# Recurrent projections: ScalarE in the written order, eight eviction tiles for the keys, squares in the keys' own tiles, decay weights in ring slots

## The chip, the cores and the metric

The kernel runs on one core of a Trainium2 chip. A core has five engines that run side by side and meet only through semaphores: TensorE (PE in the profile; PEld is its weight load), VectorE (DVE), ScalarE (ACT), GpSimd (POOL) and SyncE (SP), whose queue issues every DMA of this kernel. The metric is the device time of one execution in microseconds (us), taken as the median of several runs.

## What is computed

Two post-norm layers over 512 tokens of 1024 channels. Each layer is a half-step SwiGLU, a token mixer, and another half-step SwiGLU. The first mixer is a neighbourhood attention, the second a two-directional RWKV-7 recurrence. The change lies in the projections that feed the recurrence:

```python
xx = 0.5 * (x_prev + x_next) - x
xr, xw, xk, xv, xa, xg = (x + xx * mix[i] for i in range(6))
r = xr @ w_rkv[0]
k = xk @ w_rkv[1]
wl = w0 + tanh(xw @ w1) @ w2            # one per direction z
decay = exp(-exp(-softplus(-wl) - 0.5))
a = sigmoid(a0 + (xa @ a1) @ a2)
g = sigmoid(xg @ g1) @ g2
kk = (k * k_k) / norm(k * k_k)          # norm per head of 64 channels
```

## The kernel before, in words

**Numbers and tiles.** Activations lie with 128 channels on the partitions and the 512 tokens along a row, so 1024 channels are eight chunks, `c` or `o` = 0 to 7. To keep fp32 accuracy a large operand is split into a rounded part (ScalarE's copy to fp32r) and the rest (a subtraction on VectorE or GpSimd, line 276 after line 275). A product is then three matmuls, `mm3`, lines 285 to 287. Small products stay in plain fp32 (lines 676, 775, 781, 817).

**The stage.** `rwkv_project` runs once, between the third SwiGLU and the recurrence. It first mixes the keys' input into the split tiles `mk` (tag xT, two buffers), then:

1. multiplies the keys: eight weight blocks of 128 rows, each against all eight banks `acc[o]`; the last block finishes the banks one by one;
2. evicts each bank twice on ScalarE: `store` (line 705) copies it to an eviction tile from `evac`, which SyncE writes to `d_k`, and line 748 squares it into `sqs[o]` for the norm;
3. makes two low-rank products, `rank(0)` for the decay (`pw`) and `rank(1)` for `a` (`pa`), line 676;
4. applies a tanh to `pw` (line 752, which needs another activation table) and splits the result into `wh[z]` (lines 760 to 763);
5. splits the decay weights `w2[z]` (lines 719 to 723: a load, two roundings on ScalarE, two subtractions on VectorE, for z = 0 and 1);
6. multiplies the first 128 receptance channels, `receptance`, line 775: chunks 0 to 3, then the sums of squares `ss` per head (line 781, reading `sqs`), then chunks 4 to 7. Their inputs `t` come from VectorE (line 712) in four buffers of tag tmp;
7. multiplies the decays of direction 0 (`decays(0)`, lines 798 to 802: two matmuls, a tanh on ScalarE, a scaling on VectorE, a store to `d_lw`), the first part of the gate's second block (line 817), the decays of direction 1, the gate's hidden layer (`rank(2)`, then `tail`/`hidden`, lines 830 to 837), and four chunks of the gate itself (lines 841 to 846). `scan.begin` and `scan.front` (lines 1130 to 1420) are interleaved: they load `ah`, `k`, `r`, `lw`, `iv` back and prepare the first head pair of the recurrence.

After the stage the recurrence begins with matmuls of line 1113, whose operand `xs` SyncE loads behind the gate's four stores.

**What sets the order.** Inside `manual_schedule(engines=...)` the named engines run their instructions in the order in which the code issues them; for the others a scheduler chooses. In the block from line 735 on, PE and VectorE are manual (`MANUAL_MIX`), ScalarE is scheduled. SyncE and GpSimd are always scheduled. Each engine and SyncE's queue run strictly in their order, so an instruction that waits holds those behind it. A tile of a tag with n buffers waits until an earlier tile of the tag is no longer used. `ring` has 11 slots of 128 x 2048 elements, `raw` two per pool, with a second pool `spares` that alternates with it during this stage. `evac` goes round four tiles of 128 x 512 (one ring slot) during the keys' eviction and round eight from line 753 on.

## Time and profile before

| what | value |
|---|---|
| median of 3 runs | 2206.18 us (2203.84 to 2210.39) |
| the profiled execution: its time, its span | 2205.93 us, 2204.1 us |
| mean granted TensorE clock in it | 0.996 of full speed |
| PE busy | 2161.4 us |
| GpSimd, VectorE, ScalarE busy | 1398.9, 1056.8, 959.7 us |

The profile is one execution. Its time stands 0.25 us from the median of the runs, and 1.8 us of it lie outside the span. A row of the timeline gives an instruction or a run of like instructions: start, length, engine, line, output and input, and in brackets the idle time of its engine before it and what ended that. One plain fp32 matmul of 512 columns appears as two records. The granted clock is the share of TensorE's full clock that the hardware let through.

### The profile page before, as it was taken

How to read it: one execution, taken by the hardware profiler on the slowest of the kernel's cores; microseconds unless marked ns; L12 is line 12 of the kernel's file. 1: busy time of each engine (PE TensorE's matmuls, PEld its weight loads, DVE VectorE, ACT ScalarE, POOL GpSimd, SP SyncE). 2: the span in 40 equal slices, each digit the busy share in tenths (PEclk: the TensorE clock that was granted, in tenths of full speed). 3: DMA queues.
4: the chain of work that ended last, by engine and by line, in shares of the span. 5: the costliest groups of instructions: out<-in, count | busy, mean ns of one | idle time of the engine just before them, and what ended most of it. 6: DMA issues, size and time to landing. Idle time of an engine off the chain costs nothing.

```text
span 2204.1 us, 35069 instructions
## 1 busy us (share of the span) xinstructions
PE 2161.4 (98%) x13808; PEld 1698.6 (77%) x13808; DVE 1056.8 (48%) x1535; ACT 959.7 (44%) x1684; POOL 1398.9 (63%) x1226
## 2 busy tenths in 40 slices
PE   9999999999999999999999999999999999999998
PEld 8888888887888888888888875536666557888876
DVE  3223355367433333743333578635888545233345
ACT  3333345377333333443333443537777533333333
POOL 5988855555488877487888541045777713877753
PEclk9999999999999999999999999999999999999999
DMA  7444463432344444554444543864545653444443
GB/s 207 150 152 148 141 227 98 123 96 75 111 149 143 143 142 130 196 163 141 146 148 141 205 147 118 277 163 122 146 128 136 182 161 108 139 142 135 143 164 124
DMA packets 348628, 325.64 MB, mean 148 GB/s; under 512 B 48464, under 2 KB 277328, under 8 KB 348464
## 3 DMA queue, kind: packets, MB, share of 16 engines
q1 hardware_dynamic: 348464, 323.41, 47.5%
q8 instruction: 108, 1.77, 0.3%
q14 instruction: 56, 0.46, 0.1%
HBM read 261.22 MB, written 45.88 MB: 139 GB/s over the span
## 4 chain that ended last, share of the span: by engine, by line
PE 88%; DVE 3%; ACT 3%; DMA 2%; issue 2%; POOL 1%; SPq 1%; DVEq 0%; ACTq 0%; POOLq 0%
PE bank L286 17%; PE bank L285 17%; PE bank L287 17%; PE bank L921 16%; PE bank L348 4%; PE a L1113 3%; PE g L1441 1%; PE y L1113 1%; PE bank L1306 1%; PE m L1113 1%; PE m L1627 1%; PE g L1113 1%; PE c L1609 1%; PE g L1464 1%; PE y L1640 1%
## 5 line engine op out<-in xcount | busy, mean ns | idle before, releaser
L276 POOL TENSOR_TENSOR w<-raw,w 128x1024 fp32r<-128x1024 f32 x198 | 486.0, 2456 | 228.7 <-ACT w L275 221.3
L285 PE MATMUL bank<-xT,w 128*128 128x512 f32 x1264 | 493.9, 391 | 0.0
L286 PE MATMUL bank<-xT,w 128*128 128x512 f32 x1264 | 492.8, 390 | 0.0
L287 PE MATMUL bank<-xT,w 128*128 128x512 f32 x1264 | 492.4, 390 | 0.0
L275 ACT ACTIVATE w<-raw 128x1024 fp32r<-128x1024 f32 x202 | 213.2, 1058 | 318.8 <-POOL ts L892 131.0
L492 DVE SCALAR_TENSOR_TENSOR ar<-bank,tmp 128x512 f32<-128x512 f32 x88 | 60.9, 692 | 570.0 <-PE bank L287 558.4
L287 PEld LDWEIGHTS bank<-xT,w 128*128 128x128 f32 x1264 | 237.4, 188 | 49.5
L285 PEld LDWEIGHTS bank<-xT,w 128*128 128x128 f32 x1264 | 237.4, 188 | 48.8
L286 PEld LDWEIGHTS bank<-xT,w 128*128 128x128 f32 x1264 | 237.5, 188 | 48.1
L921 PE MATMUL bank<-wx,an 128*128 128x512 f32 x792 | 187.6, 390 | 0.0
L921 PEld LDWEIGHTS bank<-wx,an 128*128 128x128 f32 x792 | 148.7, 188 | 31.1
L921 PE MATMUL bank<-w,ring 128*128 128x512 f32 x720 | 169.1, 391 | 2.7 <-POOL w L276 2.6
L276 POOL TENSOR_TENSOR wx<-ra,wx 128x512 fp32r<-128x512 f32 x132 | 167.0, 1291 | 3.0 <-ACT wx L275 3.0
L1548 POOL TENSOR_TENSOR tm<-qs,zs 128x126 f32<-128x126 f32 (+22 forms) x248 | 106.1, 428 | 95.5 <-issue 41.1
L276 DVE TENSOR_TENSOR ring<-ar,ring 128x1024 fp32r<-128x1024 f32 x44 | 124.8, 2837 | 83.3 <-ACT ring L275 83.2
L921 PEld LDWEIGHTS bank<-w,ring 128*128 128x128 f32 x720 | 134.9, 188 | 32.3 <-POOL w L276 3.5
L490 ACT ACTIVATE tmp<-bank 128x512 f32<-128x512 f32 x88 | 52.6, 597 | 229.9 <-PE bank L287 229.9
L1550 POOL TENSOR_TENSOR zs<-zs,tm 128x126 f32<-128x126 f32 (+22 forms) x248 | 113.1, 456 | 19.4
L275 ACT ACTIVATE wx<-ra 128x512 fp32r<-128x512 f32 x132 | 82.8, 633 | 79.6 <-PE bank L921 66.6
L276 POOL TENSOR_TENSOR ring<-raw,ring 128x1024 fp32r<-128x1024 f32 x24 | 59.0, 2465 | 82.2 <-ACT ring L275 82.2
L498 DVE TENSOR_TENSOR ar<-ar 128x256 f32<-128x256 f32 x44 | 92.5, 2102 | 1.5
L276 POOL TENSOR_TENSOR w<-xT,w 128x1024 fp32r<-128x1024 f32 x25 | 65.2, 2614 | 42.5 <-ACT w L275 42.5
(358 smaller groups left out, 3976.1 us busy)
## 6 DMA issues: line engine op xcount, KB each, us to landing
raw<-in_ffn_w_in_dram SPq DMA_DIRECT2D x176, 512.0 KB, 3.9
ra<-in_ffn_w_out_dram SPq DMA_DIRECT2D x44, 1024.0 KB, 4.9
xT<-d_late SPq DMA_DIRECT2D x29, 512.0 KB, 5.1
raw<-in_w_qkv_dram SPq DMA_DIRECT2D x24, 512.0 KB, 3.9
xT<-in_ffn_w_out_dram SPq DMA_DIRECT2D x23, 512.0 KB, 4.4
d_late<-ts SPq DMA_DIRECT2D x44, 256.0 KB, 3.3
d_late<-ra SPq DMA_DIRECT2D x44, 256.0 KB, 2.0
xs<-ar SPq DMA_DIRECT2D x64, 128.0 KB, 2.6
```

Of the source, the lines that this page charges most:

```text
L275: self.hi = self.nc.scalar.activation(h, raw, AF.Copy).ins
L276: self.lo = (eng or self.nc.vector).tensor_tensor(l, raw, h.bitcast(F32), ALU.subtract).ins
L285: nc.tensor.matmul(out, wh, xh, start=start, stop=False)
L286: nc.tensor.matmul(out, wh, xl, start=False, stop=False)
L287: nc.tensor.matmul(out, wl, xh, start=False, stop=stop)
L348: nc.tensor.matmul(acc[t, h], a, u[:, i, h * 512 : (h + 1) * 512], start=first and n == 0, stop=last and n == 2)
L492: nc.vector.scalar_tensor_tensor(raw[:, 3:7:3] if j else raw[:, 0:8:7], halves_of(pu), 0.5, halves_of(s), ALU.mult, ALU.mult)
L498: nc.vector.tensor_tensor(a(2), a(1), a(0), ALU.subtract)
L921: self.nc.tensor.matmul(acc, lhs, u[:, i], start=bool(first) and m == 0, stop=last and m == 2, skip_group_check=more)
L1113: self.nc.tensor.matmul(out[hs], w[:, hs], x, start=start, stop=stop)
L1548: nc.gpsimd.tensor_tensor(tv, qs[:, s, 0:s].rearrange("p (a o) -> p a o", o=1).broadcast_to([P, s, n]), zs[:, s : s + 1, c0:].broadcast_to ...
L1550: nc.gpsimd.tensor_tensor(zs[:, 0:s, c0:], zs[:, 0:s, c0:], tv, ALU.add)
```

## The change

ScalarE joins the manual engines of the block, so it runs its instructions as the code issues them. The second eviction tile set is appended ahead of the keys' eviction, so that `evac` goes round eight tiles there. The squares go into one of the two xT buffers that held the keys' split operand, and `rows[2]` (`grows`) into the other, as before. The two decay weight units take ring slots, and the unit for z = 0 is issued ahead of the tanh, after the mixing of `low_rank(2, ...)`; the one for z = 1 follows the split of `wh`. The eviction of `pa` and the load and split of `ug` (the gate's weights) move ahead of the second half of the receptance.

```diff
-            with self.tc.manual_schedule(engines=MANUAL_MIX):
+            with self.tc.manual_schedule(engines=MANUAL_SCAN):
...
-                sqs = [q[:, c, :] for q in (quarters(), quarters()) for c in range(4)]
+                spent = [self.sb.tile([P, 4 * D], F32, name="xT", tag="xT", bufs=2) for _ in range(2)]
+                sqs, grows = ([x[:, c * S : (c + 1) * S] for c in range(ND)] for x in spent)
+                rows.append(grows)
+                evs.append(quarters())
                 for o in range(ND):
                     store(dram["rkv"][1][:, o, :], acc[o])
                     nc.scalar.activation(sqs[o], acc[o], AF.Square, scale=self.col(C_KK, o))
 
                 pw = rank(0)
+                rs = raws(0, dram["xr"])
+                soon = [next(rs) for _ in range(ND // 2)]
+                low_rank(2, g1[:, :P], 5)
+                decay_units = [decay_unit(self.ring(), 0)]
                 wt = evac()
                 nc.scalar.activation(wt, pw, AF.Tanh)
-                evs.append(quarters())
-                rs = raws(0, dram["xr"])
-                soon = [next(rs) for _ in range(ND // 2)]
-                units, grows = self.sb.tile([P, 4 * D], F32R, name="xT", tag="xT", bufs=2), self.sb.tile([P, 4 * D], F32, name="xT", tag="xT", bufs=2)
-                rows.append([grows[:, c * S : (c + 1) * S] for c in range(ND)])
-                low_rank(2, g1[:, :P], 5)
                 for z in range(2):
...
-                decay_units = [decay_unit(units[:, z * 2 * D : (z + 1) * 2 * D], z) for z in range(2)]
+                decay_units.append(decay_unit(self.ring(), 1))
...
                 pa = rank(1)
+                store(dram["ah"], pa)
...
-                store(dram["ah"], pa)
+                ug = self.load_unit(g2[:P, :], ring=True, eng=nc.vector)
                 receptance(soon)
...
-                ug = self.load_unit(g2[:P, :], ring=True, eng=nc.vector)
```

PE's and GpSimd's instructions stand as before. VectorE takes the two subtractions of the decay weights for z = 0 ahead of the split of `wh` instead of behind it, and the subtraction of `ug` ahead of the eight mixings into `xraw` instead of behind the reciprocal. On SyncE's queue the load of `ug`'s weights moves ahead of the first stores to `d_xr`, and the eight stores to `d_k` stand together. ScalarE is shown at three places. In the rows an underscore number is a buffer's; line numbers after the change are one less up to line 741 or differ by a few below it.

The first place is the end of the keys' eviction, before the change (`bank_10008` to `bank_10010` are the last three banks of keys, `raw_10303` and `raw_10309` the decay weights of z = 0 and 1):

```order
L705 ACTIVATE ring_9918<-bank_10008 128x512
L748 ACTIVATE ring_10236<-bank_10008,cols_246 128x512
L720 ACTIVATE xT_10284<-raw_10303 128x1024
L722 ACTIVATE xT_10284<-raw_10303 64x1024
L705 ACTIVATE ring_9918<-bank_10009 128x512
L748 ACTIVATE ring_10236<-bank_10009,cols_246 128x512
L720 ACTIVATE xT_10284<-raw_10309 128x1024
L722 ACTIVATE xT_10284<-raw_10309 64x1024
L705 ACTIVATE ring_9918<-bank_10010 128x512
L748 ACTIVATE ring_10236<-bank_10010,cols_246 128x512
L752 ACT_TABLE_LOAD
L752 ACTIVATE ring_9918<-bank_10261 128x512
```

The same place after the change (`raw_10293` is now z = 0's weights, `bank_10318` is `pa`):

```order
L704 ACTIVATE ring_10237<-bank_10009 128x512
L750 ACTIVATE xT_10235<-bank_10009,cols_246 128x512
L704 ACTIVATE ring_9918<-bank_10010 128x512
L750 ACTIVATE xT_10235<-bank_10010,cols_246 128x512
L719 ACTIVATE ring_10292<-raw_10293 128x1024
L721 ACTIVATE ring_10292<-raw_10293 64x1024
L758 ACT_TABLE_LOAD
L758 ACTIVATE ring_9918<-bank_10262 128x512
L762 ACTIVATE ring_9919<-ring_9918 64x512 x4
L719 ACTIVATE ring_10308<-raw_10309 128x1024
L721 ACTIVATE ring_10308<-raw_10309 64x1024
L704 ACTIVATE ring_9918<-bank_10318 128x512
```

The roundings for z = 0 moved from between the evictions to behind them, and those for z = 1 behind the tanh and its split.

The second place is the end of the receptance, before (`bank_10327` is `pr`, `bank_10385` and `bank_10391` the first decays, `ring_10462` is `ug`):

```order
L705 ACTIVATE ring_9918<-bank_10327 128x512
L275 ACTIVATE ah_10373<-ring_10374 128x512
L280 ACTIVATE gt_10371<-raw_10467 96x512
L800 ACTIVATE ring_10271<-bank_10385 128x512
L275 ACTIVATE ring_10462<-raw_10461 128x1024
L280 ACTIVATE ring_10466<-raw_10467 96x512
L800 ACTIVATE ring_10271<-bank_10391 128x512
```

After the change these roundings stand between the two directions' decays (`bank_10432` is the last of z = 0, `bank_10473` the first of z = 1):

```order
L801 ACTIVATE ring_9918<-bank_10432 128x512
L819 ACTIVATE ring_10315<-bank_10448 128x512
L274 ACTIVATE ah_10378<-ring_10379 128x512
L274 ACTIVATE a2u_10460<-a2r_10446 128x256
L279 ACTIVATE ring_10466<-raw_10467 96x512
L279 ACTIVATE gt_10376<-raw_10467 96x512
L801 ACTIVATE ring_10237<-bank_10473 128x512
```

The rounding of `ug` is gone from here; it now stands right behind the eviction of `pa`.

The third place is the gate's hidden layer, before (`gh` is its first 128 rows, `ring_9920` its split):

```order
L800 ACTIVATE ring_10271<-bank_10515 128x512
L832 ACTIVATE gh_10370<-bank_10525 128x512
L280 ACTIVATE gt_10371<-ring_10315 96x512
L1386 ACTIVATE ring_10374<-bank_10544 128x512
L1388 ACTIVATE ring_10374<-bank_10544 128x512
L1393 ACTIVATE ring_10374<-bank_10551,cols_246 128x512
L1407 ACTIVATE pcs_10458<-ring_10374 64x8 x2
L275 ACTIVATE ring_9920<-gh_10370 128x512
```

After:

```order
L832 ACTIVATE ring_10315<-bank_10523 96x512
L279 ACTIVATE gt_10376<-ring_10315 96x512
L832 ACTIVATE gh_10375<-bank_10525 128x512
L274 ACTIVATE ring_9920<-gh_10375 128x512
L1386 ACTIVATE ring_10379<-bank_10544 128x512
L1388 ACTIVATE ring_10379<-bank_10544 128x512
L1393 ACTIVATE ring_10379<-bank_10551,cols_246 128x512
L1407 ACTIVATE pcs_10463<-ring_10379 64x8 x2
```

The rounding of the hidden layer now follows its activation directly; five instructions of the recurrence's preparation stand behind it.

More of the change, by code (lines that the diff above doesn't have):

```diff
@@ L50 @@
 MANUAL = {mybir.EngineType.PE}
-MANUAL_MIX = {mybir.EngineType.PE, mybir.EngineType.DVE}
 MANUAL_NORM = {mybir.EngineType.Activation, mybir.EngineType.DVE}
```

## The prediction

> **What bounds the kernel now.** The first page first: the span and the busy shares.

> ```profile
> span 2204.1 us, 35069 instructions
> PE 2161.4 (98%) x13808; PEld 1698.6 (77%) x13808; DVE 1056.8 (48%) x1535; ACT 959.7 (44%) x1684; POOL 1398.9 (63%) x1226
> ```

> TensorE is busy for all but 42.7 us, so a faster other engine can only win what PE idles, or what its clock loses. No PE instruction is added, removed or moved. Next the waits, between the end of the keys' products and the first matmuls of the recurrence.

> ```profile
> PE bank L775 <- DVE tmp L712: 4.8, 1, 4.8
> PE y L1113 <- DMA xs<-in_w_rkv_dram: 2.4, 1, 2.4
> PE bank L285 <- ACT ring L275: 2.1, 1, 2.1
> PE bank L817 <- ACT ring L800: 0.6, 1, 0.6
> ```

> Each row has the total, the count and the longest wait in us. PE's longest is for VectorE's `tmp`. The timelines of ScalarE, VectorE and PE show what makes those late:

> ```profile
> 1346.90 0.60 ACT L705 ACTIVATE ring<-bank 128x512 f32<-128x512 f32 x1 [8.73 <-PE bank L287]
> 1350.54 0.74 ACT L748 ACTIVATE ring<-bank,cols 128x512 f32<-128x512 f32 x1
> 1356.31 0.60 ACT L705 ACTIVATE ring<-bank 128x512 f32<-128x512 f32 x1 [5.04 <-DMA d_k<-ring]
> 1358.42 1.07 ACT L720 ACTIVATE xT<-raw 128x1024 fp32r<-128x1024 f32 x1
> 1364.43 1.28 ACT L752 ACT_TABLE_LOAD   x1
> 1365.73 0.60 ACT L752 ACTIVATE ring<-bank 128x512 f32<-128x512 f32 x1
> 1366.36 2.57 ACT L762 ACTIVATE ring<-ring 64x512 fp32r<-64x512 f32 x4
> ...
> 1353.26 5.39 DVE L681 SCALAR_TENSOR_TENSOR xT<-ring,cols,xraw 128x512 f32<-128x512 f32 x8
> 1369.68 1.22 DVE L721 TENSOR_TENSOR xT<-raw,xT 64x1024 fp32r<-64x1024 f32 x1
> 1374.63 2.74 DVE L712 SCALAR_TENSOR_TENSOR tmp<-ring,cols,xraw 128x512 f32<-128x512 f32 x4
> ...
> 1351.47 13.89 PE L676 MATMUL bank<-ring 128*128 128x512 f32 x32
> 1365.20 3.60 PE L775 MATMUL bank<-tmp,wr 128*128 128x512 f32 x8
> 1368.72 1.92 PE L781 MATMUL bank<-ring,heads 128*32 128x512 f32 x16
> 1375.44 5.93 PE L775 MATMUL bank<-tmp,wr 128*128 128x512 f32 x8 [4.79 <-DVE tmp L712]
> 1380.80 4.24 PE L798 MATMUL bank<-xT,ring 128*128 128x512 f32 x16
> ```

> Four pairs of copy and square fill the four eviction tiles by 1351.28; ScalarE then stands still until a store to `d_k` has landed. With two decay roundings in between, the tanh comes at 1365.73, though `rank(0)` had ended halfway through the 13.89 us of line 676, at 1358.42. VectorE holds its four `tmp` mixings behind the tanh's split and four subtractions, and PE waits 4.79 us. Eight records of line 775 then take 5.93 us instead of 3.60: the clock.

> ```profile
> 1375.40:1379.40 4.00, 3.96 (x5) 1.85 (x6) 4.00 (x7) 0.00 (x0) 0.00 (x0) 0.50 0.79 217
> 1402.90:1407.30 4.40, 4.17 (x10) 3.11 (x11) 4.33 (x8) 1.72 (x3) 0.00 (x0) 0.61 0.75 251
> 1415.90:1418.30 2.40, 0.07 (x2) 0.00 (x0) 2.30 (x4) 2.21 (x6) 0.00 (x0) 1.00 0.96 285
> ```

> The column behind the five engines is the granted clock. It stood at 0.50 for 4 us after the first wait and at 0.61 on average after the second (2.12 us at line 285), but at 1.00 through the third, of 2.4 us.

> **The change, term by term.**

> *Eviction and tanh.* The wait for `d_k` goes: eight tiles take eight copies. The eight pairs follow each other at the pace of the first four, (1351.28 - 1346.90) / 4 = 1.1 us, to about 1355.7; the two roundings of z = 0 (1.07 us, each starting 0.95 behind the other) end at 1357.7. The squares' new buffer held chunks 0 to 3 of the keys' operand, read long before; the other buffer is free when the keys' products end, at about 1351.6, before VectorE writes it at 1353.26, as now. The table load waits for `rank(0)`, so the tanh runs from 1359.9 to 1360.5 (before: 1365.73), the four roundings to 1363.1, those of z = 1 to 1365.1.

> *VectorE.* After the mixings end at 1358.65 it subtracts for z = 0 (2 x 1.22, to 1361.1), splits the tanh (its last subtraction waits for ScalarE's 1363.1, so to 1363.8), subtracts for z = 1 to 1366.6. The first `tmp` buffer is free when PE has read it, at about 1366.2; the four mixings end at 1369.6. PE needs the first at 1370.6, and it is there from 1367.3: 3.3 us of cover. The wait of 4.79 us goes, and with it the idle time that halved the clock: the second half of the receptance costs what the first did. Line 775's first half ends at 1368.80, 0.08 us after line 781 starts; with the same overlap line 781 takes 1.84 us, and then 3.52 us (1368.72 - 1365.20) lead to line 798 at 1374.08 instead of 1380.80: **-6.7 us**.

> *Decays.* PE's 0.62 us in front of line 817 came from a bank that ScalarE freed late, with roundings of `ah`, `gt` and `ug` between its first tanhs. These now stand behind the eight tanhs or before the receptance: **-0.6 us**. The cost: four roundings (about 2 us) now lie in front of direction 1's tanhs, which start at 1382.7 instead of 1380.9. PE has free banks until its eighth product there, so it reaches the next small product at about 1384 without a wait.

> *The hidden layer.* Before and after:

> ```profile
> 1399.20 0.60 ACT L832 ACTIVATE gh<-bank 128x512 f32<-128x512 f32 x1 [2.71 <-PE bank L676]
> 1402.19 0.63 ACT L275 ACTIVATE ring<-gh 128x512 fp32r<-128x512 f32 x1
> 1401.04 0.43 DVE L833 TENSOR_SCALAR gh<-gh 128x512 f32<-128x512 f32 x1
> 1402.86 0.69 DVE L276 TENSOR_TENSOR ring<-gh,ring 128x512 fp32r<-128x512 f32 x1 [1.39 <-ACT ring L275]
> 1403.60 0.61 PE L286 MATMUL bank<-ring 128*128 128x512 f32 x1 [0.23 <-DVE ring L276]
> 1408.75 1.06 PE L1383 MATMUL a<-tri,lw 128*128 128x128 f32 x8
> ```

> From the activation's start to line 286 it takes 4.40 us, since five other activations stand before the rounding. With the rounding next: 0.60 + 0.43 + 0.63 + 0.69 and some 0.15 between them, 2.5 us: **-1.9 us**. PE then idles 0.8 us in two pieces instead of 2.35, too little for the clock to fall by these rows. In the window from 1402.90 PE was busy for 4.17 us at 0.61 of the clock; at full clock that is 2.5: **-1.6 us**. The five activations move back by 0.6 us; the first PE instruction that needs one of them is line 1383's, 5 us behind line 286.

> [...]

> *SyncE's queue.* The `ug` load moves ahead of the `d_xr` stores and waits for GpSimd to free a buffer of key weights.

> ```profile
> 1338.25 2.61 POOL L276 TENSOR_TENSOR w<-raw,w 128x1024 fp32r<-128x1024 f32 x1 [10.64 <-ACT w L275]
> 1392.98 0.33 SPq L813 DMA_DIRECT2D d_iv<-ring  x1
> 1404.13 0.92 SPq L1368 DMA_DIRECT2D lw<-d_lw  x2
> 1385.03 3.48 ACT L800 ACTIVATE ring<-bank 128x512 f32<-128x512 f32 x7
> 1389.61 3.35 DVE L812 RECIPROCAL ring<-ring 128x512 f32<-128x512 f32 x1
> lw<-d_lw SPq DMA_DIRECT2D x4, 256.0 KB, 3.1
> ```

> Even the last key weight is done at 1340.86, 10 us before the first store: nothing. The load of `lw` for line 1383 followed the `d_iv` issue by 11.15 us. The store follows the reciprocal, which ended at 1392.96. Now the eight tanhs (0.5 us apart) run from 1374.7 to 1378.8, VectorE's last scaling and the norm's first step take it to 1379.9, and 3.35 us to 1383.3. So `lw` is issued at about 1394.5 and lands 3.1 us later (median, last row), at 1397.6; PE comes to line 1383 at 1397.95: no wait, but no cover either. The load of `xs` hangs on the gate's fourth store and moves with it, so the 2.4 us at line 1113 stay.

> **Sum:** 6.7 + 0.6 + 1.9 + 1.6 = 10.8 us. Against the profiled execution, 2205.93 us, that is **2195.1 us**; the runs' median stands 0.25 above that execution, within their scatter, so I take the same number for it. The later stages keep their order, and PE was 98% busy, so I let the gain through whole. A measurement of this kernel can tell about 0.3%, 6.6 us, from no change.

> **The rivals.**

> *A. The short gap isn't what halves the clock in the second stretch.* For it: the third gap, of 2.4 us, left it at 1.00. Against it: the drop begins right behind the gap of 2.12. Then the 1.6 us stay: 2196.7 us. [...] Chance 0.10.

> *B. The transfers give some of it back.* Over this stretch the DMA engines are busy for 0.75 to 0.96 of the time (the window rows' share), and the same bytes now move in some 11 us less.

> ```profile
> DMA to landing us min/median/max: 2.8/3.4/5.5
> DMA to landing us min/median/max: 5.9/7.9/9.6
> ```

> The first row is of tile `d_lw` and its reloads, the second of the `xs` and `vt` weight loads. If `lw` takes 5.5 us, PE waits 2.2 at line 1383, and a halved clock for 4 us costs 2 more; of this the 2.4 at line 1113 absorb as much: 1.8 lost. If `xs` takes 9.6 instead of 5.9 (the row's ends), another 3.7 are lost, and up to 2 if line 1113 then starts at half clock. Together up to 7.5, and some 3 where only one of these comes: 2198 us, at worst 2202.6. Chance 0.15.

> *C. The gain is absorbed.* The recurrence behind it, or a wait that I don't see in the new order, takes most of it: the first term alone must shrink by more than half. What would do it: the cover of 3.3 us at `tmp` is gone because ScalarE or VectorE starts the chain 5 us later than I have it. Then about 2202 to 2206 us. The rows against it: nothing before the tanh waits but `rank(0)`. Chance 0.11.

> *D. Slower.* In the written order the rounding of `ah` holds all of direction 1's tanhs, and `ah` comes back from memory behind `pa`'s store on SyncE's queue. PE runs out of banks, and each us late is a us lost.

> ```profile
> 1369.58 0.33 SPq L706 DMA_DIRECT2D d_ah<-ring  x1
> 1371.77 0.33 SPq L1136 DMA_DIRECT2D ring<-d_ah  x1
> ```

> Before, it took from the store's issue at 1369.58 to the reload's at 1371.77 and, with the 3.1 us of `lw`, a load of the same size, to 1374.9. From an eviction of `pa` that ends at 1365.9 that makes 1371.2, and ScalarE wants it at 1381: 10 us of cover. The gain is used up when the reload lands at about 1394 (1381, the 2 us that PE has in hand, and 10.8), 28 us behind the eviction instead of some 6; a slower time needs more, say 1404: 2216 us. Chance 0.03.

> That ScalarE does not follow the written order can be left out: the rows of the change show it.

> **The numbers.** The forecast has 0.61. Its own range is 2192.7 (the 2.4 us at line 1113 vanish too) to 2197. Left out of the range may be 0.2: it reaches from 2191.5, with 1 us for the runs' scatter, over A and nearly all of B to 2201.5, and leaves out C and D. Faster by more than 6.6 us: forecast, A, and two thirds of B, 0.81. Within 6.6: the rest of B and most of C, 0.15. Slower by more: D and a remainder, 0.04.

> **What would show it.** Right: no wait for `d_k` at the keys' eviction; the tanh right behind `rank(0)`; line 776 (now) without a wait and its second half in 3.6 us; a granted clock of 1.00 throughout; the rounding of `gh` within 1.1 us of its activation's start. Wrong: a wait of PE at the receptance or at line 1383, half clock in either stretch, or a wait at line 1113 longer by what was won.

## The result, and the profile after

The changed kernel takes 2196.96 us (median of 5 runs, 2192.57 to 2197.62) against 2206.18 us in the same session. The two medians differ by 9.2 us. The ratio of all these runs is 0.9951, with a 95% interval of 0.9936 to 0.9966: faster by 10.8 us (2206.18 x 0.0049), with 7.5 to 14.1 by the interval's ends. A second set of six runs of the same kernel, with its own runs of before, gave 2194.19 and a ratio of 0.9942 (0.9929 to 0.9955). The profiled execution took 2197.62 us.

The first page of after, its span and busy shares:

```profile
span 2195.8 us, 35075 instructions
PE 2160.7 (98%) x13808; PEld 1696.8 (77%) x13808; DVE 1052.7 (48%) x1535; ACT 959.0 (44%) x1684; POOL 1400.7 (64%) x1226
```

TensorE does the same work; its idle time fell from 42.7 to 35.1 us. All of PE's waits of 0.2 us or more from 1340 to 1500 us, after the change (total, count, longest):

```profile
PE y L1113 <- DMA xs<-in_w_rkv_dram: 2.5, 1, 2.5
PE a L284 <- ACT v L1480: 0.6, 1, 0.6
PE bank L285 <- DVE ring L275: 0.2, 1, 0.2
PE bank L284 <- ACT ring L274: 0.2, 1, 0.2
```

The waits at the receptance and ahead of the gate's first part are gone, the hidden layer's is 0.4 us in two pieces, and `xs` stays. ScalarE's timeline shows the tanh at its new time and the rounding of `gh` behind its activation:

```profile
1355.31 1.19 ACT L719 ACTIVATE ring<-raw 128x1024 fp32r<-128x1024 f32 x1
...
1358.57 1.28 ACT L758 ACT_TABLE_LOAD   x1 [1.22 <-PE bank L675]
1359.87 0.60 ACT L758 ACTIVATE ring<-bank 128x512 f32<-128x512 f32 x1
...
1391.47 0.60 ACT L832 ACTIVATE gh<-bank 128x512 f32<-128x512 f32 x1 [1.79 <-PE bank L675]
1392.57 0.63 ACT L274 ACTIVATE ring<-gh 128x512 fp32r<-128x512 f32 x1 [0.49 <-DVE gh L833]
```

The tanh comes 5.86 us earlier than before, and now waits for nothing but `rank(0)` and the table load. PE's timeline over the same stretch:

```profile
1370.59 3.70 PE L776 MATMUL bank<-tmp,wr 128*128 128x512 f32 x8
1373.72 4.24 PE L799 MATMUL bank<-ring 128*128 128x512 f32 x16
1377.89 1.92 PE L818 MATMUL bank<-xT,ring 128*32 128x512 f32 x16
...
1393.25 0.49 PE L284 MATMUL bank<-ring 128*128 128x512 f32 x1 [0.22 <-ACT ring L274]
...
1397.56 1.09 PE L1383 MATMUL a<-tri,lw 128*128 128x128 f32 x8
...
1407.31 5.26 PE L1113 MATMUL y<-az,xs 128*64 128x512 f32 x16 [2.49 <-DMA xs<-in_w_rkv_dram]
```

The receptance's second half takes 3.70 us instead of 5.93, and line 1383 comes 11.2 us earlier than before (1408.75 - 1397.56). But the 16 records of line 1113 behind the wait for `xs` take 5.26 us, where the kernel before took 3.65.

For all kernels of the experiments below, this table sets the k-th matmul record of PE against the k-th of before and subtracts the starts (added matmuls left out). The executions' difference at 1346 us, near the end of the keys (-0.01 to 1.58 us, also between two executions of one kernel), is taken off. "Receptance" is its second half, "decays" the first product behind it, "gate" the first behind the hidden layer, line 1113 its first record and "behind it" the record after its 32. Columns are us gained on before:

| kernel | receptance | decays | gate | line 1383 | line 1113 | behind it |
|---|---|---|---|---|---|---|
| after | 4.86 | 7.09 | 9.64 | 11.20 | 11.05 | 9.45 |
| a2_again | 4.86 | 7.08 | 9.64 | 10.93 | 10.85 | 10.85 |
| p1_four_tiles | 3.91 | 6.13 | 8.08 | 8.12 | 7.82 | 7.82 |
| p2_act_scheduled | 4.86 | 7.08 | 8.87 | 8.54 | 8.62 | 8.62 |
| p3_decay_late | 4.86 | 7.08 | 8.92 | 9.30 | 9.36 | 7.75 |
| u1_ug_late | 4.86 | 7.08 | 4.17 | 5.73 | 6.01 | 6.01 |
| t1_rounding_back | 4.86 | 7.08 | 7.84 | 7.94 | 6.33 | 4.63 |
| p4_order_alone | 3.36 | 5.58 | 0.80 | 2.35 | 2.40 | 2.40 |
| q1_order_ug | 3.38 | 5.60 | 7.89 | 7.74 | 7.43 | 5.74 |
| b1_before_busy | -0.06 | 2.17 | 1.96 | 2.10 | 2.03 | 2.03 |
| f1_busy_at_xs | 4.86 | 7.08 | 9.64 | 11.04 | 11.04 | 10.82 |
| x1_xs_first | 4.86 | 7.08 | 9.64 | 11.01 | 11.98 | 11.42 |
| x2_xs_first_busy | 4.86 | 7.09 | 9.64 | 10.97 | 11.78 | 11.41 |

Each row is one execution. The changed kernel's two, `after` and `a2_again`, agree to 0.01 us up to the gate and differ by 0.2 to 1.4 us behind it, so small differences count in the first three columns alone.

### The profile page after: what moved, and what is told of

It is laid out like the page before. It is cut to its first block, busy times and chain, and to the rows that moved or that the text cites. A ratio compares the mean times of both kernels' runs of the same rounds, so it can differ in the third digit from the quotient of the medians.

```text
span 2195.8 us, 35075 instructions
## 1 busy us (share of the span) xinstructions
PE 2160.7 (98%) x13808; PEld 1696.8 (77%) x13808; DVE 1052.7 (48%) x1535; ACT 959.0 (44%) x1684; POOL 1400.7 (64%) x1226
## 4 chain that ended last, share of the span: by engine, by line
PE 90%; ACT 2%; DMA 2%; DVE 2%; issue 1%; POOL 1%; SPq 1%; DVEq 0%; ACTq 0%; POOLq 0%
PE bank L285 17%; PE bank L284 17%; PE bank L286 17%; PE bank L921 17%; PE bank L347 4%; PE a L1113 3%; PE g L1441 1%; PE y L1113 1%; PE bank L1306 1%; PE m L1627 1%; PE bank L675 1%; PE c L1609 1%; PE m L1113 1%; PE g L1113 1%; PE g L1464 1%
## 5 line engine op out<-in xcount | busy, mean ns | idle before, releaser
L275 POOL TENSOR_TENSOR w<-raw,w 128x1024 fp32r<-128x1024 f32 x198 | 487.5, 2464 | 228.5 <-ACT w L274 221.2
L285 PE MATMUL bank<-xT,w 128*128 128x512 f32 x1264 | 492.3, 389 | 0.0
L286 PE MATMUL bank<-xT,w 128*128 128x512 f32 x1264 | 491.8, 389 | 0.0
L286 PEld LDWEIGHTS bank<-xT,w 128*128 128x128 f32 x1264 | 237.3, 188 | 49.9
L285 PEld LDWEIGHTS bank<-xT,w 128*128 128x128 f32 x1264 | 237.3, 188 | 48.1
L275 POOL TENSOR_TENSOR wx<-ra,wx 128x512 fp32r<-128x512 f32 x132 | 167.3, 1298 | 2.9 <-ACT wx L274 2.9
L275 DVE TENSOR_TENSOR ring<-ar,ring 128x1024 fp32r<-128x1024 f32 x44 | 122.0, 2774 | 80.3 <-ACT ring L274 80.2
L275 POOL TENSOR_TENSOR ring<-raw,ring 128x1024 fp32r<-128x1024 f32 x24 | 58.9, 2463 | 81.8 <-ACT ring L274 81.8
L275 POOL TENSOR_TENSOR w<-xT,w 128x1024 fp32r<-128x1024 f32 x25 | 64.0, 2568 | 45.1 <-ACT w L274 45.1
## 6 DMA issues: line engine op xcount, KB each, us to landing
d_late<-ts SPq DMA_DIRECT2D x44, 256.0 KB, 3.3
d_late<-ra SPq DMA_DIRECT2D x44, 256.0 KB, 2.0
```

Of the source, the lines that this page charges most:

```text
L275: self.lo = (eng or self.nc.vector).tensor_tensor(l, raw, h.bitcast(F32), ALU.subtract).ins
L285: nc.tensor.matmul(out, wh, xl, start=False, stop=False)
L286: nc.tensor.matmul(out, wl, xh, start=False, stop=stop)
```

## The experiments

### What one execution of the clock says: a2_again and b1_before_busy

The changed kernel again, unedited.

> The changed kernel once more, unedited, to see how much of its profile recurs. In the first profiled execution the granted clock fell to half for three stretches of 3.41 us (from 1407.16 at line 1113, from 1731.43, and from 2141.03 in the last stage), though PE's gaps ahead of two of them were no longer than in the kernel before, where the same gaps cost nothing. If the gap's length decides, the same stretches come back in the same places, and line 1113's 16 records take 5.26 us again. If it depends on where the gap lies on a grid of 3.41 us that runs on its own, the half stretches come elsewhere or not at all in this execution, and line 1113 takes anything between 3.65 and 5.3 us, with the receptance and the hidden layer unchanged within 0.1 us. The median should be 2193 to 2198 us either way.

In the windows of the trace below, the first of each pair is the 3.41 us in which PE waits for `xs`, the second what follows (start and end, length, then PE, PEld, DVE, ACT, POOL busy, the granted clock, and what the DMA engines did). The half clock came in stretches of 3.41 us, at the receptance of before in two on end. Within one execution their starts lie whole numbers of 3.413 us (409.60 / 120) apart, to 0.04 us: 30.72 us in before (from 1373.13 to 1403.85, nine), 324.27 and 409.60 us in the changed kernel (from 1407.16 to 1731.43 and 2141.03, 95 and 120). Windows of that length laid end to end from such a stretch make the grid meant here. First the changed kernel's first profiled execution:

```profile
1403.75:1407.16 3.41, 1.07 (x16) 0.88 (x16) 2.31 (x4) 3.16 (x8) 0.00 (x0) 1.00 0.98 304
1407.16:1410.57 3.41, 3.26 (x8) 1.14 (x10) 2.25 (x4) 0.31 (x2) 0.00 (x0) 0.50 1.07 399
```

And its second:

```profile
1401.39:1404.80 3.41, 2.38 (x20) 1.35 (x18) 1.46 (x4) 3.19 (x8) 0.00 (x0) 1.00 0.92 244
1404.80:1408.21 3.41, 2.04 (x10) 0.89 (x12) 3.31 (x6) 1.58 (x6) 0.00 (x0) 1.00 1.02 369
```

PE's row of line 1113 in the second execution:

```profile
1406.17 3.65 PE L1113 MATMUL y<-az,xs 128*64 128x512 f32 x16 [2.39 <-DMA xs<-in_w_rkv_dram]
```

The same code waited 2.49 and 2.39 us. Once nearly all of the gap lay in one window, in which PE was busy for 1.07 us, and the next ran at half clock; once it lay across two, busy for 2.38 and 2.04, and the clock stayed. Line 1113's 16 records took 5.26 and 3.65 us. So the place of the gap on the grid decides here, not its length alone. The windows of before fit:

```profile
1369.71:1373.13 3.42, 0.94 (x12) 0.03 (x4) 3.39 (x3) 0.00 (x0) 0.00 (x0) 1.00 0.73 234
1373.13:1379.96 6.83, 4.52 (x6) 1.94 (x7) 6.78 (x11) 0.00 (x0) 0.00 (x0) 0.50 0.67 186
...
1400.44:1403.85 3.41, 1.05 (x4) 0.43 (x3) 2.00 (x4) 3.06 (x7) 0.00 (x0) 1.00 1.02 387
1403.85:1407.27 3.42, 3.42 (x9) 2.67 (x9) 3.35 (x7) 1.06 (x2) 0.00 (x0) 0.50 0.67 211
...
1414.09:1417.50 3.41, 1.88 (x19) 1.12 (x17) 1.50 (x3) 3.16 (x9) 0.00 (x0) 1.00 0.93 252
1417.50:1420.90 3.40, 2.56 (x12) 1.05 (x14) 3.06 (x5) 1.09 (x4) 0.00 (x0) 1.00 1.03 382
```

The gaps of 4.79 and 2.12 us left 0.94 and 1.05 us of work in a window, the one of 2.4 us was cut in two. At the receptance the half clock had begun at 1373.13, 2.3 us before the wait ended.

So windows with 0.94 to 1.07 us of PE work were enough for a half clock behind them, and a gap of 2.12 us was long enough to leave such a window.

`b1_before_busy` measures the clock alone, in the kernel before:

```diff
                 store(dram["ah"], pa)
+                self.busy(self.bank(), 20)
                 receptance(soon)
```

> The kernel before the change with 20 added matmuls, whose results nothing reads, in the receptance's wait for tmp (4.79 us in the profile of before). This measures the clock's share of the first term by itself. Theory: the wait stays (tmp is late as before), but with PE busy the clock does not fall: the eight records of line 775's second half take 3.6 us instead of 5.93, and all behind is 2.3 us earlier than in the kernel before; of the first term's 6.7 us 4.4 are then the wait and 2.3 the clock. Rival: the 5.93 us have another cause (the operands' arrival one by one: the four mixings end some 0.7 us apart, 2.74 us for four); then the second half takes 5 us or more at a granted clock of 1.00 and nothing is won.

PE's timeline of it (line 385 is the added work, two records each):

```profile
1369.70 4.73 PE L385 MATMUL bank<-ident 128*128 128x128 f32 x40
1374.61 3.70 PE L775 MATMUL bank<-tmp,wr 128*128 128x512 f32 x8 [0.18 <-DVE tmp L712]
```

`tmp` is as late as before (-0.06 us), the second half takes 3.70 us, and what follows comes 2.17 us earlier. So of the 7.08 us of the receptance 4.86 are the wait and 2.2 the clock, as the first theory had it. The median fell by less, to 2204.94 us, ratio 0.9992 (0.9982 to 1.0001), not to be told from no change: in the profiled execution 1.6 of the 2.0 us are lost again in the recurrence, in several steps of about 1 us or less.

### Which edit carries the receptance: p1, p2, p3, p4

`p1_four_tiles`, from the changed kernel:

```diff
-                evs.append(quarters())
                 for o in range(ND):
                     store(dram["rkv"][1][:, o, :], acc[o])
                     nc.scalar.activation(sqs[o], acc[o], AF.Square, scale=self.col(C_KK, o))
+                evs.append(quarters())
```

> The changed kernel with four eviction tiles for the keys again instead of eight; all else stays. Theory: the written order carries the first term, the tiles little of it. ScalarE stands still for d_k again until about 1356.3, four pairs of 1.1 us and the two roundings of z = 0 (2 us) take it to 1362.8, the table load and the tanh to 1364.7, the four roundings to 1367.3; VectorE's first tmp mixing ends at about 1371.2, and PE, which wants it at 1370.6, waits 0.5 to 1 us, too little for a half clock: behind the receptance 0.5 to 1 us less gain than the changed kernel, about 10.2 us at line 1383. Rival: the tiles carry it. Then the wait for tmp is 4 us or more, the clock falls behind it as before, and 4 to 6.7 us of the gain are gone.

ScalarE's timeline, then three of PE's waits:

```profile
1355.23 0.60 ACT L704 ACTIVATE ring<-bank 128x512 f32<-128x512 f32 x1 [5.07 <-DMA d_k<-ring]
...
1362.76 0.60 ACT L758 ACTIVATE ring<-bank 128x512 f32<-128x512 f32 x1
```

```profile
PE a L1383 <- DMA lw<-d_lw: 1.4, 1, 1.4
PE bank L776 <- DVE tmp L711: 0.9, 1, 0.9
PE bank L284 <- ACT ring L274: 0.7, 1, 0.7
```

ScalarE stands 5.07 us for `d_k` again and the tanh is 4.0 us later (1362.76 against 1359.87, with the 1.12 us between the two executions at 1346 us added), yet PE waits 0.9 us, without a half clock (2.22 us are gained from the second half's start to the decays, 6.13 - 3.91, as in the changed kernel, 7.09 - 4.86): the theory. What it did not hold is what the delay costs later: the rounding of `gh` keeps PE waiting 0.7 us instead of 0.2, and `lw` lands 1.4 us late, so that 8.1 us, not 10.2, are left at line 1383. Median 2196.20 us, ratio 0.9954 (0.9938 to 0.9971).

`p2_act_scheduled` leaves ScalarE to the scheduler (`MANUAL_SCAN` becomes PE and VectorE alone).

> The changed kernel with ScalarE's order left to the scheduler again; eight tiles, the squares' place, the ring slots and the moved code stay. Theory: the code's new places with eight tiles are enough for the receptance (the tanh within 1 us of rank(0)'s end or of the table load, no wait of PE for tmp, second half in 3.6 us), so 7 us of the gain stay; the rounding of the hidden layer gets two activations ahead of it, and PE idles some 1 us more there: about 1 us (0.5 to 2) behind the changed kernel at line 1383. Rival: the written order is what removes the wait; then PE waits 2 us or more at the receptance and half or more of the gain is gone.

The receptance gains all of its 7.08 us without the written order; the rounding of `gh` behind two other activations costs 0.8 us more at the gate (9.64 - 8.87), as expected. Then PE waits 1.7 us for `lw`, so that line 1383 is 2.66 us behind the changed kernel (11.20 - 8.54), more than the 0.5 to 2 expected. 2196.12 us, ratio 0.9957 (0.9942 to 0.9971).

`p3_decay_late` puts both decay units behind the split of `wh`.

> The changed kernel with both decay units behind the split of wh, so that no rounding stands between the keys' evictions and the tanh. Theory: the tanh waits for rank(0) and the table load anyway, so it starts when it did (1359.9, within 0.3 us); the roundings and subtractions of z = 0, some 2 us more behind it, are taken out of the cover at tmp, 3.3 us in the forecast, and about 1 us of it is left: no wait at the receptance, and line 799 within 0.3 us of the changed kernel. Rival: the place ahead of the tanh matters. Then PE waits 0.5 to 2 us for tmp, and all behind it is so much later.

The receptance is the changed kernel's to 0.01 us: the place ahead of the tanh buys nothing there. But the hidden layer and `lw` come later (waits of 0.7 and 1.0 us): 9.30 us at line 1383, which the theory had not looked at. 2197.34 us, ratio 0.9962 (0.9949 to 0.9976).

`p4_order_alone` is the kernel before with one word:

```diff
-            with self.tc.manual_schedule(engines=MANUAL_MIX):
+            with self.tc.manual_schedule(engines=MANUAL_SCAN):
```

> The kernel before with one word changed: ScalarE runs the block in the order in which the code issues it. Four eviction tiles, the decay weights' roundings behind the tanh and its split, the load of ug late, as the code of before has them. Theory: most of the change is this word. The tanh no longer stands behind the two roundings between the evictions; PE waits about 1.2 us (0.5 to 2) at the receptance and its clock stays at 1.00 there, the rounding of the gate's hidden layer follows its activation, and at line 1383 the kernel is some 9.7 us (8.5 to 10.5) ahead of before, against 11.2 for the whole change. Rival: without the new places of the roundings the order gives little, because the keys' evictions still wait for d_k's stores: a wait of 3 us or more at the receptance with a half clock behind it, and 2 to 5 us of gain at line 1383.

Neither theory. The receptance went as the first had it (PE waits 1.4 us, the second half behind it takes the 3.70 us of the full clock, 5.58 us gained at the decays), and then nearly all was lost at a new place. PE's longest wait, ScalarE's and SyncE's timelines:

```profile
PE bank L830 <- ACT ring L800: 5.3, 1, 5.3
```

```profile
1381.56 0.62 ACT L275 ACTIVATE ah<-ring 128x512 fp32r<-128x512 f32 x1
1387.27 0.42 ACT L275 ACTIVATE a2u<-a2r 128x256 fp32r<-128x256 f32 x1 [5.09 <-DMA a2r<-in_a_dram]
```

```profile
1379.39 4.66 SPq L802 DMA_DIRECT2D d_lw<-ring  x8
1384.14 0.61 SPq L1350 DMA_DIRECT2D a2r<-in_a_dram  x1
```

SyncE has the load of `a2r` behind the eight stores of `d_lw`, ScalarE's written order has the rounding of `a2u` ahead of all of direction 1's tanhs, and PE runs out of banks for 5.3 us. Behind that, two records of line 830 take 2.02 us (1.02 in the changed kernel) and eight of line 676 4.52 (3.60 in the changed kernel at a clock of 1.00). It ends at 2204.11 us, ratio 0.9989 (0.9980 to 0.9999).

### What keeps the written order from stalling: u1 and q1

In the changed kernel that load goes out at 1375.85, ahead of the stores:

```profile
1375.85 0.61 SPq L1350 DMA_DIRECT2D a2r<-in_a_dram  x1
1376.57 5.29 SPq L803 DMA_DIRECT2D d_lw<-ring  x8
```

The one edit that could move it is the place of `ug`:

```diff
-                ug = self.load_unit(g2[:P, :], ring=True, eng=nc.vector)
                 receptance(soon)
...
                 scan.fetch(0, 0)
+                ug = self.load_unit(g2[:P, :], ring=True, eng=nc.vector)
```

> The changed kernel with the load and split of ug at its old place, behind the preparation for the second half of the gate; all else stays. In the kernel with the written order alone PE waited 5.32 us at line 830 for banks: ScalarE stood 5.09 us at the rounding of a2u, whose load SyncE issued only at 1384.14, behind the eight d_lw stores; in the changed kernel the same load goes out at 1375.85, ahead of them. Theory: it is the place of ug that puts this load on the one or the other side of the stores, and the written order that makes direction 1's tanhs wait for it. So with ug late the receptance stays as in the changed kernel (no wait, 3.6 to 3.7 us for the second half), but ScalarE stands 4 to 6 us at a2u's rounding, PE waits 4 to 6 us at line 831, with half clock for some us behind it, and at line 1383 the kernel is 6 to 9 us behind the changed one: about 2203 us. Rival: that wait came from the later receptance of the order-alone kernel (its wait of 1.43 us for tmp, its tanhs later by as much). Then it is 1 us or less here, only the one rounding of ug (1 us) stands ahead of direction 1's tanhs, and the kernel is within 1.5 us of the changed one.

PE's longest wait, ScalarE's and SyncE's timelines of `u1_ug_late`:

```profile
PE bank L830 <- ACT ring L800: 3.5, 1, 3.5
```

```profile
1383.13 0.42 ACT L274 ACTIVATE a2u<-a2r 128x256 fp32r<-128x256 f32 x1 [3.31 <-DMA a2r<-in_a_dram]
```

```profile
1374.72 5.12 SPq L802 DMA_DIRECT2D d_lw<-ring  x8
1379.94 0.74 SPq L1350 DMA_DIRECT2D a2r<-in_a_dram  x1
```

The receptance is untouched, and the stall is back: PE waits 3.5 us at line 830 and loses 5.5 us at line 1383 (11.20 - 5.73); behind the wait two records of line 830 take 1.40 us instead of 1.02, and 16 of line 675 8.47 instead of 7.03. The theory had 4 to 6 and 6 to 9: right in kind, too large. 2201.25 us, ratio 0.9977 (0.9968 to 0.9986).

`q1_order_ug` is `p4_order_alone` with `ug` ahead of the receptance's second half, and nothing else.

> The kernel before with two of the edits: ScalarE in the written order, and the load and split of ug ahead of the receptance's second half. Four eviction tiles, the squares and the decay weights' tiles and places stay as before. Theory: these two carry nearly all. PE waits 1.2 to 1.6 us for tmp at the receptance as with the order alone, without a half clock; no wait at line 831; the hidden layer's rounding follows its activation; the load of lw comes somewhat late (PE waits 0.5 to 1.5 us for it). At line 1383 the kernel is 8 to 9.5 us ahead of before, and its median is 2195 to 2199 us, not to be told from the changed kernel's. Rival: without the eight tiles and the earlier decay roundings a wait of 3 us or more stays at line 775 or 831, and the time is 2200 us or more.

Two of PE's waits:

```profile
PE a L1383 <- DMA lw<-d_lw: 1.5, 1, 1.5
PE bank L775 <- DVE tmp L712: 1.4, 1, 1.4
```

No wait at line 830; 1.4 us for `tmp`, 1.5 for `lw`, 7.74 us gained at line 1383 (a little under the 8 expected). 2198.09 us, ratio 0.9967 (0.9955 to 0.9979): the two edits carry about two thirds by the first set of the changed kernel (0.33% of 0.49) and by line 1383 (7.74 us of 11.20), somewhat more than half by the second set (0.33% of 0.58).

### The hidden layer: t1_rounding_back

```diff
-                    else:
-                        self.split(gh[0][:, 0, :], gh[0][:, 1, :], raw)
                 start = scan.front(0, 0)
                 for _ in range(3):
                     next(start)
+                self.split(gh[0][:, 0, :], gh[0][:, 1, :], scan.hidden[:, 0, :])
```

> The changed kernel with the split of the gate's hidden layer behind the recurrence's first three preparation steps again, so that five activations stand ahead of the rounding as before. This prices the term of 1.9 us and asks for its 1.6 us of clock. Theory: PE idles some 2 us at line 285 instead of 0.45 in two pieces, and line 286 comes 1.5 to 2 us later than in the changed kernel; whether the clock falls behind that depends on the place on the grid of 3.41 us, so line 1383 is 1.5 to 3.5 us later. Rival: the term isn't the order of the activations (the bank or the other operand comes late anyway): then line 286 moves by less than 0.5 us.

PE's timeline and two windows of it:

```profile
1393.89 0.50 PE L284 MATMUL bank<-ring 128*128 128x512 f32 x1 [2.02 <-ACT ring L274]
```

```profile
1391.00:1394.41 3.41, 1.37 (x6) 0.57 (x4) 1.80 (x4) 2.59 (x6) 0.00 (x0) 1.00 0.74 282
1394.41:1397.82 3.41, 3.21 (x8) 2.53 (x9) 1.61 (x4) 1.30 (x2) 0.00 (x0) 0.50 0.53 160
```

The order alone costs 1.80 us at the gate (9.64 - 7.84), and the half clock behind it 1.5 more at line 1383 (3.26 in all). Behind that the wait for `xs` grew to 4.0 us: from its issue to line 1113's start it took 7.98 us (1410.87 - 1402.89) instead of 6.29 in the changed kernel. Why was not tried. 2197.78 us, ratio 0.9966 (0.9954 to 0.9978).

### The wait that stays: f1, x1, x2

`f1_busy_at_xs` adds nine matmuls on the identity, whose results nothing reads, ahead of line 1113's first products.

> The changed kernel with nine added matmuls in the wait for xs, whose results nothing reads; they keep PE busy where it stood still for 2.49 us ahead of line 1113. Theory: the half clock behind this gap costs what the matched records lose there, 1.4 to 1.6 us; with PE busy the clock stays at 1.00, line 1113's 16 records take 3.65 us instead of 5.26, and it begins when it began (within 0.3 us), so the gain over the kernel before is 11 us behind line 1113 instead of 9.8. Rival: the halving has nothing to do with PE's standing still (a throttle for another reason); then line 1113's records take some 5.3 us again, or the added matmuls themselves run at half clock and line 1113 starts later.

PE's timeline (line 384 is the added work):

```profile
1404.19 2.27 PE L384 MATMUL y<-ident 128*128 128x128 f32 x18
1406.57 3.87 PE L1113 MATMUL y<-az,xs 128*64 128x512 f32 x16
```

The clock stayed at 1.00 (from 1403 to 1410) and line 1113 began with the same 11.04 us of gain, as the theory said; but it does so in `a2_again` without the filler. 2194.14 us, ratio 0.9942 (0.9929 to 0.9955).

`x1_xs_first` issues the first `az` chunk and `xs` ahead of the mask and the ones.

> The changed kernel, with the loads of xs and of the first az chunk issued ahead of those of the mask and the ones on SyncE's queue. In the changed kernel the mask is issued at 1399.26, xs at 1401.02, and PE waits 2.49 us for xs at line 1113. Theory: the wait is set by the place of xs on the queue, so it shrinks by the two issues passed, some 1.2 us, to 1.0 to 1.5 us, and the half clock of line 1113 goes with it (16 records in 3.65 us instead of 5.26): 2.5 to 3 us sooner than the changed kernel behind line 1113, about 2194 us by the profiled execution. Rival: the transfer, not the place on the queue, is the limit (the DMA engines are busy for most of this time), xs lands when it landed, and the wait stays at 2.3 to 2.6 us; then only the grid decides the clock, and the time is the changed kernel's, 2197 us.

SyncE's row of `xs` in the changed kernel, then SyncE's and PE's timelines of this one:

```profile
1401.02 0.43 SPq L1199 DMA_DIRECT2D xs<-in_w_rkv_dram  x1
```

```profile
1398.53 0.46 SPq L1199 DMA_DIRECT2D xs<-in_w_rkv_dram  x1
```

```profile
1404.79 3.95 PE L1113 MATMUL y<-az,xs 128*64 128x512 f32 x16 [1.34 <-DMA xs<-in_w_rkv_dram]
```

From the issue of `xs` to line 1113's start it takes 6.26 us, in the changed kernel 6.29 (1407.31 - 1401.02): the place on the queue sets the wait, which halves. Yet the median is 2194.99 us, ratio 0.9946 (0.9931 to 0.9962).

`x2_xs_first_busy` has both edits, with five matmuls.

> The changed kernel with both edits at line 1113: xs and the first az chunk ahead of the mask and the ones on SyncE's queue, and five added matmuls, whose results nothing reads, in the 1.3 us of wait that this left. Each edit alone gave 2195.0 and 2194.1 us as medians, against 2194.2 and 2197.0 for the changed kernel's two sets of runs. Theory: the edits add up behind line 1113 (11.9 to 12.3 us ahead of before there, against 10.9 to 11.0 for the changed kernel, and never a half clock at line 1113), so the median falls by 1 to 2.5 us below the changed kernel's two medians' mean of 2195.6: 2193 to 2194.6 us. Rival: what is won there is lost to the clock in the recurrence, whose half-clock stretches (3.4 to 6.8 us near 1730, now and then 3.4 near 2140) come with the place on the grid; then the trace shows the 12 us behind line 1113, but the median stays at 2194.6 to 2197 us.

It is 11.78 us ahead at line 1113 and 11.41 behind it, a little under the 11.9 expected, and line 1113's 16 records took 4.02 us there, against 5.26 with the half clock. The median is 2194.29 us, ratio 0.9941 (0.9928 to 0.9955): in the range of the first theory, but not to be told from the changed kernel's second set. The three have medians from 2194.1 to 2195.0, and none is shown to be faster than the change.

## Why the prediction was right, point by point

**Receptance, -6.7 us.** Measured 7.08 (1380.80 - 1373.72; 7.09 in the table, with the 0.01 us between the two executions): 4.86 of wait and 2.2 of clock, which `b1_before_busy` gives by itself. The tanh was forecast for 1359.9 and came at 1359.87, the last `tmp` for 1369.6 and came at 1369.6. The 0.4 us beyond the forecast are PE's: from the second half's start to line 799 it took 3.13 us, not 3.52.

**But its cause was told too narrowly.** "The wait for `d_k` goes" is true and is not what carries the term: with that wait in place (`p1_four_tiles`) 6.13 of 7.08 us are won, without the written order (`p2_act_scheduled`) all, with the order alone 5.58. The written order alone takes most of VectorE's lateness away, the tiles with the moved code do so without it, and whichever comes second finds little left. The eight tiles alone, in the kernel before, were not run.

**Decays, -0.6.** Measured 0.69: the gate's first part starts at 1377.89 and started at 1385.66, which makes 7.78 with the 0.01 us between the executions, less 7.09 at the decays. Direction 1's tanhs, forecast for 1382.7, started at 1382.25 without holding PE.

**Hidden layer, -1.9 and -1.6.** Measured 1.86 (9.64 - 7.78) and 1.56 (11.20 - 9.64). `t1_rounding_back` puts the old order back and loses 1.80 and 1.5 us. The 0.8 us of idle time that the prediction left there do not follow from its own figures (2.35 - 1.9 = 0.45), and 0.45 us came (0.22 + 0.23); its sum does not use them. Rival A, in which the 1.6 us stay, falls: the clock did fall to 0.50 behind that gap of 2.12 us, and behind the 2.02 us of `t1_rounding_back`, and without the gap it stood at 1.00.

**`lw`, no wait and no cover.** Its load was forecast for 1394.5 and went out at 1394.62; PE waited 0 in the first execution and some 0.3 us in the second. That there is no cover four kernels show: in `p1`, `p2`, `p3` and `q1` that load goes out 1.8 to 3.4 us later, counted like the table, and PE waits 1.0 to 1.7 us for it.

**The step that failed: the clock by the gap's length.** The prediction took from one row that a gap of 2.4 us leaves the clock at 1.00, so that "the 2.4 us at line 1113 stay" at no further cost. The wait stayed, at 2.49 us. In the profiled execution it now filled most of a window of 3.41 us, and line 1113 lost 1.6 us (11.05 to 9.45 in the table). Rival B had such a loss, but for a late `xs`; it came without one. So a granted clock of 1.00 throughout, one of the prediction's signs of being right, did not come in this execution; it did, up to 1729, in `a2_again`. Two more stretches of 3.41 us of half clock, from 1731 and from 2141, stand in the first execution; the one at 1731 has its like in before, the other costs 1.6 us more and is absent in the second execution. So the gain was not let through whole: 8.3 us of 11.2 reach the first execution's end, which took 2197.62 us instead of 2195.1, and 9.7 that of the second. By the medians' two differences the gain is 9.2 and 12.0 us, around the 10.8 forecast. That the ratio of the first set gives the same 10.8 is luck: its profiled execution won more than that at line 1383 and less at its end, as the windows fell. By its time alone the first median, 2196.96, fits rival A's 2196.7 better than 2195.1; it is the trace that rules A out.

**`ug`, "nothing".** As a cost that was right. But the move is worth 5.5 us at line 1383 (`u1_ug_late`), because on SyncE's scheduled queue it keeps the load of `a2r` ahead of eight stores. The prediction looked for what the moved load waits for, not for what would stand elsewhere without it.

**Rival D** gave this mechanism a chance of 0.03, with `ah` as the late operand. It didn't come in the change, since both loads were ahead of the stores. In the order-alone kernel it came with `a2u`, and took back 4.8 us between the decays and the gate (5.58 to 0.80).

## What to carry to other kernels

An order written by hand on one engine can put any load that it waits for on the critical path, as it did with `a2r` (PE waited 5.3 us in `p4_order_alone`, 3.5 in `u1_ug_late`), so look where each of those loads stands on a queue that is still scheduled, and which edit put it there. Price edits by taking one away at a time: the terms of this chain did not add up, since two edits could each remove the same wait (at the decays 6.13 us without the eight tiles, 7.08 without the written order, of 7.08). A gap's price had two parts here, the gap and the half clock behind it (at the receptance 4.86 and 2.2 us), and the second depended on where the gap fell (at line 1113, 1.6 us or nothing), so read it from several executions.

## What the runs showed of the hardware

```profile
1725.65:1729.07 3.42, 2.10 (x36) 1.44 (x34) 2.36 (x6) 2.75 (x8) 2.87 (x8) 1.00 0.80 243
1729.07:1735.90 6.83, 6.45 (x46) 3.34 (x44) 2.64 (x9) 1.50 (x5) 5.82 (x13) 0.50 0.89 321
```

Why they differ there stays open. In the table a half window costs 1.5 to 1.7 us (1.46 and 1.70 in `t1_rounding_back`, 1.60 in the changed kernel), and one more or less of them lies within the spread of one kernel's runs (2192.57 to 2197.62 us).
